# A two-layer trunk on one core: small TensorE products as alternating groups, GpSimd's arithmetic on VectorE, SwiGLU gates by tanh beside the mixers

## The chip, the cores and the metric

The kernel runs on one core of a Trainium2 chip. The metric is the device time of the program in microseconds (us). The engines are named as in the profile: PE is TensorE (PEld its weight loads), DVE is VectorE, ACT is ScalarE, POOL is GpSimd, SP is SyncE, whose queue issues the DMAs.

## The reference, cut to what matters

The input is x, 256 tokens of 1024 channels, and 256 memory tokens. Two layers are run one after the other; each is a half-weighted SwiGLU block, a mixer, and a second half-weighted SwiGLU block, each with a residual and a layer norm behind it.

```python
for i in range(DEPTH):            # 2 layers
    x = layer_norm(ALPHA * x + 0.5 * swiglu(x, ffn1...[i]), ...)
    proj = x @ w_in               # rwkv_w_in in layer 0, sb_w_in in layer 1
    mix  = rwkv7_mix(...) if i == 0 else stick_breaking_mix(...)
    heads = concatenate([mix, memory_attention(mq, mem_k, mem_v)])
    x = layer_norm(ALPHA * x + heads @ w_out[i], ...)
    x = layer_norm(ALPHA * x + 0.5 * swiglu(x, ffn2...[i]), ...)

def swiglu(x, w_gate, w_up, w_down):
    return (jax.nn.silu(x @ w_gate) * (x @ w_up)) @ w_down     # 1024 -> 2816 -> 1024
```

RWKV-7 mixing has 12 heads of 64 channels and a state of 64x64 a head, which is carried along the tokens with a decay; stick-breaking attention has 12 heads of 64 and a causal mask, and multiplies each token's weight with what earlier breaks left over; memory attention is a softmax over the 256 memory tokens with 4 heads of 64.

## The kernel before, in words

**Tiling.** The 256 tokens are two halves of 128 (`hf` 0 and 1), one token a partition. A matrix product with weights uses float32 split into a rounded high part and the rest: `piece` loads up to 128x1024 weights into a `raw` buffer, ACT makes `hi` and DVE makes `lo` = raw - hi, and each product is three fp32r products (`mm3`). There are nine `hi` and nine `lo` buffers (NPIECE) and eight `raw` ones. DVE's `lo` instructions have one line each in the profile (`lo<-raw,hi`, 128x1024).

**Feed-forward blocks.** The 2816 hidden channels are 11 blocks of 256 (`ffn_block`). A block of one half alone ("single") computes gate and up for that half with 24 products of 512 columns, gates them in `gated` (tile `h`), turns `h` with the PE (`turn_h`) and adds the down product to the accumulators of that half (`acc0` or `acc1`). A "shared" block serves both halves at once with 96 products of 256 columns and loads its weights once. A single block for each half loads the same weights twice. A single block has six weight pieces, as a shared one has.

**Order of the halves.** The two halves run out of step: while one half is in its mixer, the other half's single blocks stand beside it as work for PE. LAGS says how many blocks are single ones before and after each mixer, HEAD and HOLD and TAIL which of them run before, with, or after which step; `alternate` deals out the fill by weights in RW and SB.

**The mixers.** In `rwkv` a half is two chunks of 64 tokens (`c`), and partitions of a tile are (chunk, token) or (head parity, channel). Its products of 64 rows by 64 columns use one quarter of the PE array each. `narrow` makes head products out of `qr` and `bt`, `kq` those of `kt` and `qr`; `product` (in the loop over `_LEVELS`) inverts a triangular matrix by blocks; then a loop over the two chunks does c0 (Sk·V into `xb` and `Ov`), c1 (Tt·X into `ub`, which becomes U), the state's part (`through_state`), c3 (the new state S), and RB·U into `Ov`. In the trace Sk·V is `vn,Sk`, Tt·X is `L,Tt`, RB·U is `Lm,RB`, and the state's part is `S,qr`. In `stick` the scores z use 64 rows and 128 columns (`bn,S` and `bn,kn` in the trace), the outputs 128 rows and 64 columns. `mem_attention` has scores of 64 rows (`memKT,mq`) and outputs of 64 columns (`eT,memV`); it is called by both mixers.

**What sets the order.** Every engine runs its own queue in order. The kernel first records all operations in `Plan` (`add` with the dependencies found by `touch`, and `price` for a duration), then `order` picks, by due times, one operation after another for all engines, `improve` repeats that 24 times with shaken priorities from a random generator (SEED) and keeps the best by its own cost sheet, and `issue` writes the program in that order. So an edit to the operations or to a constant of the planner gives a new order for the whole kernel. BOOST is a bonus for the operations of a mixer's chain, SWITCH a malus for an ACT function outside the table that is loaded, AHEAD how far a queue may look ahead.

**Silu and tables.** ACT holds tables of functions; SETS in the planner has them as (Exp, Tanh), (Sigmoid, Tanh), (Ln, Exp), (Silu, Tanh). A function outside the loaded set costs a table load, which the profile shows as ACT_TABLE_LOAD.

Of the kernel before, what the change touches and what calls it, by code (L numbers as in the profile page):

```python
# [12 lines left out]
F32 = mybir.dt.float32  # L13
# [31 lines left out]
LAGS = ((5, 9), (4, 8))  # L45
# [6 lines left out]
TAIL = (3, 2)  # L52
AHEAD = dict(PE=0.0, DVE=400.0, ACT=0.0)
WAIT = 0.98
SWITCH = 392.0
BOOST = 26.25
# [46 lines left out]
class Op:  # L103
    __slots__ = ("i", "eng", "fn", "a", "k", "took", "lag", "after", "opens", "closes", "pri", "func", "port", "left",
                 "ready", "end", "users", "row", "kb", "turns", "mode", "rows", "spent", "fine")
# [18 lines left out]
SEED = 2  # L124
# [3 lines left out]
class Plan:  # L128


    def __init__(self, nc):
# [6 lines left out]
        self.index = {}  # L138
# [24 lines left out]
    def add(self, eng, fn, method, a, k):  # L163
        o = Op()
        o.i, o.eng, o.fn, o.a, o.k = len(self.ops), eng, fn, a, k
        o.pri = o.i + self.bias
        o.after = {}
# [5 lines left out]
        o.turns = [j for j, real in o.after.items() if not real]  # L173
        o.after = list(o.after)
        self.price(o, method, aps)
        self.ops.append(o)
        return o

    def touch(self, o, x, w):
# [16 lines left out]
        if psum:  # L196
            for q in range(q0, q1):
                if o.eng == "PE":
# [3 lines left out]
                    if st["pe"][q] is not None:  # L202
                        dep[st["pe"][q]] = True
# [36 lines left out]
    def price(self, o, method, aps):  # L240
        free = lambda x: int(np.prod([n for _, n in x.ap[1:]])) if len(x.ap) > 1 else 1
        sb = lambda x: x.space != PSUM
        o.func, o.port, o.row, o.kb, o.mode, o.rows = None, False, None, 0.0, None, 0
# [3 lines left out]
        if o.eng == "PE":  # L247
            out, st, mv = o.a[0], o.a[1], o.a[2]
            cols, m = free(mv), free(st)
            rows = st.ap[0][1]  # L250
            o.mode, o.rows = (rows <= 64, m <= 64), rows
            if method == "transpose":
                o.took, o.lag = 111.0, 175.0
            elif st.dtype == F32R:
                o.took, o.lag = max(cols / 2.4, m / 1.2) + 13.3, 180.0
            elif rows <= 64 and m <= 64:
                o.took, o.lag = 58.0 * max(1.0, cols / 64), 220.0
            else:
                o.took, o.lag = 2 * max(cols / 1.2, m / 1.2 + 4), 200.0
                if rows <= 64:  # L260
                    o.row = st.offset // st.ap[0][0] // 64
        elif o.eng == "ACT":
            fun = o.a[2] if len(o.a) > 2 else o.k["func"]
            o.func = {AF.Exp: "Exp", AF.Tanh: "Tanh", AF.Sigmoid: "Sigmoid", AF.Ln: "Ln", AF.Silu: "Silu"}.get(fun)
            ptr = sum(isinstance(o.k.get(x), bass.AP) for x in ("scale", "bias"))
            o.took = 95.0 + 0.845 * n + 93.0 * ptr + (92.0 if "accum_out" in o.k else 0.0)
# [28 lines left out]
    def order(self, given=()):  # L295
# [14 lines left out]
        for name, st in self.seen.items():  # L310
            if name in self.tag_of:
                ops[st["ops"][0]].opens.append(name)
                for j in set(st["ops"]):
                    ops[j].closes.append(name)
        held, self.reuse = {}, []
# [6 lines left out]
        table, landed, row = 0, 0.0, None  # L322
# [6 lines left out]
        def earliest(o):  # L329
            t = o.ready  # L330
            for n in o.opens:
                f = free[self.tag_of[n]]
                if not f:
                    return None
                t = max(t, f[0][0])
            return t

        while done < len(ops):
# [41 lines left out]
            if e == "PE":  # L380
                if t > clock["PE"] + 30:
                    t += 60.0
                if o.row is not None and row is not None and row != o.row:
                    took *= 0.55
                row = o.row
                if o.mode != mode:
                    if mode is not None:
                        t += 95.0
                        took += 108.0 * (o.a[1].dtype == F32R)
# [6 lines left out]
                share = min(o.rows, P) / P  # L396
# [111 lines left out]
    def issue(self, tc):  # L508
# [14 lines left out]
        with tc.manual_schedule():  # L523
            for _, _, o in order:
                for x in chain(o.a, o.k.values()):
# [7 lines left out]
                o.fn(*[at(x) for x in o.a], **{k: at(x) for k, x in o.k.items()})  # L533
# [3 lines left out]
def kernel(ctx, tc, const, x, mem, f1g, f1u, f1d, f2g, f2u, f2d, ln_g, ln_b, w_out, w_mem_kv,  # L537
# [60 lines left out]
    def mm3(o, sh, sl, wh, wl, start, stop):  # L598
        nc.tensor.matmul(o, sh, wh, start=start, stop=False)
        nc.tensor.matmul(o, sh, wl, start=False, stop=False)  # L600
        return nc.tensor.matmul(o, sl, wh, start=False, stop=stop)
# [13 lines left out]
    def to_T(src, dst, j0, n):  # L615

        for g in range(0, n, 4):
            m = min(4, n - g)
            pt = ps("tp")
            for i in range(m):  # L620
                nc.tensor.transpose(pt[:, i * P:(i + 1) * P], src[:, (g + i) * P:(g + i + 1) * P], ident)
# [84 lines left out]
    def ffn_block(w, c, halves):  # L706
# [42 lines left out]
        for k in range(KT):  # L749
            for f in range(2):  # L750
                for u in range(2):
                    wh, wl = (t[:, k % 2, u * FC + f * P:u * FC + (f + 1) * P] for t in gu[k // 2])
                    b = o[f][:, u * SEQ:(u + 1) * SEQ]
                    nc.tensor.matmul(b, wh, xTt[0][:, k], start=k == 0 and u == 0, stop=False)
                    nc.tensor.matmul(b, wh, xTt[1][:, k], start=False, stop=False)
                    nc.tensor.matmul(b, wl, xTt[0][:, k], start=False, stop=k == KT - 1 and u == 1)
# [36 lines left out]
    def mem_attention(hf, mqT):  # L793

        o = ps(f"acc{hf}")
        ov = o[:, :MEMW].rearrange("p (j t) -> p j t", j=2)
        rs = new(tp_, [P, 3, NMH], F32, "rs", "rs", 2)
        for p in range(2):
            sc = ps(f"acc{hf}")
            scv = sc.rearrange("p (j m) -> p j m", j=2)  # L800
            pr = slice(p * HD, (p + 1) * HD)
            two = slice(2 * p, 2 * p + 2)
            for j in range(2):
                nc.tensor.matmul(scv[:, j], mqT[pr, j], memKT[pr, j], start=True, stop=True)
# [9 lines left out]
            pt = ps("tp")  # L814
            for j in range(2):
                for m in range(2):
                    i = 2 * j + m
                    nc.tensor.transpose(pt[:, i * P:(i + 1) * P], e[:, j, m * P:(m + 1) * P], ident)
# [585 lines left out]
```

## Time and profile before

| | |
|---|---|
| median of 3 runs | 1150.29 us (1149.66 to 1152.18) |
| profiled execution | 1150.96 us, span 1149.2 us |
| PE, DVE, ACT, POOL busy | 1107.0, 932.0, 753.9, 63.6 us |
| mean granted TensorE clock | 0.990 |
| read from HBM | 301.08 MB |

Busy time is the union of an engine's instructions. Matmuls overlap in the array, so a busy PE is not a PE at its peak: for the pace of small products the start times of a run of them count, not the length of one. All instructions are issued from one line of the program (L533), so groups are told apart by their tiles: `out<-in` with the shapes, `rows*columns` of the array in front for PE.

### The profile page before, as it was taken

To read this page: it belongs to the slowest core of one execution; us is meant where nothing else is said; L and a number is where in the kernel's file an instruction comes from. 1 tells how busy PE (TensorE), PEld (TensorE's weight loads), DVE (VectorE), ACT (ScalarE), POOL (GpSimd) and SP (SyncE) were. 2 spreads that over 40 slices of the span, in tenths; PEclk is the share of its full clock that TensorE was granted. 3 is DMA by queue.
4 is the path that set the end of the run, shared out by engine and by line. 5 is a ranking of instruction groups with operands and counts; after the bars stand their busy time and mean duration, and the time that the engine had idled before them with its cause. 6 is when DMAs were issued, how large, how long until landed. Compare 5 with 4: busy or idle time off the path is not lost.

```text
span 1149.2 us, 19305 instructions
## 1 busy us (share of the span) xinstructions
PE 1107.0 (96%) x7021; PEld 932.8 (81%) x7021; DVE 932.0 (81%) x1358; ACT 753.9 (66%) x1007; POOL 63.6 (6%) x50
## 2 busy tenths in 40 slices
PE   7999999999899989999999999999999999999996
PEld 7799888877878768888887898988876776888885
DVE  5747679999799996998788955558879888997677
ACT  6545558985269863667666645447797799766562
POOL 0000000122400124000000000000100000000000
PEclk9999999999799999999999999999999999999999
DMA  9669778862658764799989986777977986999883
GB/s 353 227 233 329 259 240 306 298 211 97 207 192 290 237 184 139 238 365 342 340 272 329 315 278 191 236 226 255 368 236 247 324 284 204 369 358 298 277 281 123
DMA packets 212258, 303.42 MB, mean 264 GB/s; under 512 B 13844, under 2 KB 159424, under 8 KB 212162
## 3 DMA queue, kind: packets, MB, share of 16 engines
q1 hardware_dynamic: 212162, 302.18, 77.6%
q8 instruction: 55, 0.90, 0.3%
q14 instruction: 41, 0.34, 0.1%
HBM read 301.08 MB, written 1.05 MB: 263 GB/s over the span
## 4 chain that ended last, share of the span: by engine, by line
PE 77%; DVE 8%; DMA 5%; ACT 5%; issue 2%; POOL 1%; SPq 0%; DVEq 0%; ACTq 0%; POOLq 0%
PE ps_30r L533 24%; PE ps_29r L533 22%; PE ps_25r L533 7%; PE ps_26r L533 7%; PE ps_28r L533 6%; PE ps_27r L533 6%; PE ps_3r L533 3%; PE ps_2r L533 2%; ACT L533 1%; DVE Tt_366r L533 1%; DVE x L533 1%; DVE lo_17r L533 1%; DVE lb_506r L533 1%; DVE lo_14r L533 1%; DMA raw_24r<-in_sb_w_in_dram 1%
## 5 line engine op out<-in xcount | busy, mean ns | idle before, releaser
L533 ACT ACTIVATE h_33r<-ps_30r 128x256 f32<-128x256 f32 (+1 forms) x51 | 21.4, 420 | 55.2 <-PE ps_30r L533 53.1
L533 ACT ACTIVATE h_32r<-ps_29r 128x256 f32<-128x256 f32 (+1 forms) x49 | 19.9, 407 | 42.5 <-PE ps_29r L533 38.7
L533 ACT ACT_TABLE_LOAD x33 | 42.3, 1283 | 3.7 <-DVE rs_798r L533 1.7
L533 DVE TENSOR_TENSOR h_33r<-h_33r,ps_30r 128x256 f32<-128x256 f32 x40 | 16.7, 418 | 25.0 <-ACT h_33r L533 24.6
L533 DVE TENSOR_TENSOR h_32r<-h_32r,ps_29r 128x256 f32<-128x256 f32 x42 | 17.6, 420 | 22.6 <-ACT h_32r L533 22.3
L533 POOL COPY gup_134r<-h_32r 128x256 f32<-128x256 f32 (+1 forms) x2 | 5.5, 2755 | 371.3 <-ACT h_32r L533 352.5
L533 PE MATMUL ps_30r<-lo_8r,xTh 128*128 128x512 f32 (+1 forms) x48 | 18.8, 392 | 0.3 <-DVE lo_8r L533 0.3
L533 PE MATMUL ps_30r<-lo_17r,xTh 128*128 128x512 f32 (+1 forms) x42 | 16.8, 400 | 1.2 <-DVE lo_17r L533 1.2
L533 PE MATMUL ps_2r<-cst,x 128*128 128x128 f32 x48 | 9.4, 301 | 8.2 <-DMA x<-in_x_dram 5.4
L533 ACT ACTIVATE hi_37r<-raw_18r 128x1024 fp32r<-128x1024 f32 x12 | 12.7, 1056 | 6.8 <-issue 2.0
L533 ACT ACTIVATE hi_40r<-raw_36r 128x1024 fp32r<-128x1024 f32 x11 | 11.6, 1057 | 8.4 <-DMA raw_36r<-in_sb_w_in_dram 3.8
L533 ACT ACTIVATE hi_16r<-raw_15r 128x1024 fp32r<-128x1024 f32 x11 | 11.6, 1059 | 8.1 <-PE ps_27r L533 2.4
L533 PE MATMUL ps_30r<-hi_16r,xTh 128*128 128x512 f32 (+1 forms) x44 | 16.8, 382 | 0.0
L533 PE MATMUL ps_30r<-lo_35r,xTh 128*128 128x512 f32 x40 | 16.7, 418 | 0.0
L533 ACT ACTIVATE hi_40r<-raw_39r 128x1024 fp32r<-128x1024 f32 x14 | 14.8, 1054 | 2.7 <-PE ps_28r L533 1.5
L533 ACT ACTIVATE hi_22r<-raw_9r 128x1024 fp32r<-128x1024 f32 x12 | 12.7, 1060 | 5.7 <-PE ps_30r L533 3.1
L533 PE MATMUL ps_30r<-hi_7r,xTh 128*128 128x512 f32 (+1 forms) x42 | 16.4, 390 | 0.0
L533 PE MATMUL ps_30r<-hi_16r,xTl 128*128 128x512 f32 (+1 forms) x44 | 16.3, 371 | 0.0
L533 PE MATMUL ps_30r<-hi_7r,xTl 128*128 128x512 f32 (+1 forms) x42 | 16.2, 385 | 0.0
L533 DVE TENSOR_TENSOR xTl<-ps_2r,xTh 128x512 fp32r<-128x512 f32 (+1 forms) x15 | 10.0, 669 | 7.2 <-ACT xTh L533 7.1
L533 PE MATMUL ps_30r<-lo_14r,xTh 128*128 128x512 f32 (+1 forms) x40 | 15.4, 385 | 0.0
L533 PE MATMUL ps_29r<-hi_22r,xTl 128*128 128x512 f32 x38 | 15.3, 404 | 0.0
(1998 smaller groups left out, 4606.0 us busy)
## 6 DMA issues: line engine op xcount, KB each, us to landing
raw_24r<-in_ffn_w_down_dram SPq DMA_DIRECT2D x25, 512.0 KB, 5.1
raw_18r<-in_ffn_w_gate_dram SPq DMA_DIRECT2D x41, 256.0 KB, 4.1
raw_18r<-in_ffn_w_up_dram SPq DMA_DIRECT2D x41, 256.0 KB, 5.1
raw_12r<-in_ffn_w_gate_dram SPq DMA_DIRECT2D x36, 256.0 KB, 4.3
raw_12r<-in_ffn_w_up_dram SPq DMA_DIRECT2D x36, 256.0 KB, 6.2
raw_15r<-in_ffn_w_gate_dram SPq DMA_DIRECT2D x36, 256.0 KB, 4.0
raw_15r<-in_ffn_w_up_dram SPq DMA_DIRECT2D x36, 256.0 KB, 4.8
raw_39r<-in_ffn_w_gate_dram SPq DMA_DIRECT2D x36, 256.0 KB, 4.9
```

What stands on the lines that cost most here:

```text
L533: o.fn(*[at(x) for x in o.a], **{k: at(x) for k, x in o.k.items()})
```

## The change

1. `together` binds products into one unit of the plan, issued without anything in between; the three products of `mm3`, the transposes into one bank and the small products of a step are such units. Inside the small units the order alternates between parts of the array: `narrow` and `kq` go over (head parity, chunk) as (0,0), (1,1), (1,0), (0,1) into two banks; memory scores, z and the outputs alternate the head parity; c0 is done for both chunks at once, alternating chunks; RB·U of chunk 0 alternates with Tt·X of chunk 1.
2. The state's x part goes into banks of its own as 12 products of 64x64 for a chunk instead of 6 of 128x64 into `xb`, and DVE adds it to X.
3. All arithmetic and copies of POOL move to DVE; POOL keeps its memsets.
4. Beside a mixer a single block is gated with tanh: silu(g)·u = 0.5·g·(1 + tanh(g/2))·u, one ACT instruction and two DVE instructions instead of Silu and one multiply. BESIDE says where.
5. Planner: `price` knows the places of a product in the array; the special price for alternating rows goes; constants as in the diff.

```diff
-LAGS = ((5, 9), (4, 8))
+LAGS = ((5, 9), (5, 8))
...
-TAIL = (3, 2)
-AHEAD = dict(PE=0.0, DVE=400.0, ACT=0.0)
+TAIL = (2, 2)
+AHEAD = dict(PE=100.0, DVE=400.0, ACT=0.0)
 WAIT = 0.98
-SWITCH = 392.0
-BOOST = 26.25
+SWITCH = 49.0
+BOOST = 18.375
+BESIDE = (True, False)
...
-SEED = 2
+SEED = 201
...
+    @contextmanager
+    def together(self):
+        self.bundle = []
+        yield
+        o, self.bundle = self.bundle[0], None
+        self.close(o)
...
     def mm3(o, sh, sl, wh, wl, start, stop):
-        nc.tensor.matmul(o, sh, wh, start=start, stop=False)
...
+        with nc.together():
+            nc.tensor.matmul(o, sh, wh, start=start, stop=False)
...
         def gated(dst, g, u):
-            nc.scalar.activation(dst, g, AF.Silu)
-            nc.vector.tensor_tensor(dst, dst, u, ALU.mult)
+            if beside:
+                nc.scalar.activation(dst, g, AF.Tanh, scale=0.5)
+                nc.vector.scalar_tensor_tensor(dst, dst, 1.0, g, ALU.add, ALU.mult)
+                nc.vector.scalar_tensor_tensor(dst, dst, 0.5, u, ALU.mult, ALU.mult)
+            else:
...
     def mem_attention(hf, mqT):
+        banks = [ps(f"acc{hf}").rearrange("p (j m) -> p j m", j=2) for p in range(2)]
+        with nc.together():
+            for j in range(2):
+                for p, pr in enumerate(rows):
+                    nc.tensor.matmul(banks[p][:, j], mqT[pr, j], memKT[pr, j], start=True, stop=True)
...
+        with nc.together():
             for j in range(2):
                 for m in range(2):
+                    for p, pr in enumerate(rows):
+                        h = 2 * j + p
+                        nc.tensor.matmul(ov[pr, j], memV[:, m, h * HD:(h + 1) * HD], turned_e[p][:, j, m], start=m == 0, stop=m == 1)
...
-            nc.gpsimd.tensor_tensor(Lm, L, bc(lvl[:, l], 1, [P, NH, C]), ALU.mult)
+            nc.vector.tensor_tensor(Lm, L, bc(lvl[:, l], 1, [P, NH, C]), ALU.mult)
...
+        with nc.together():
+            for i in range(NH):
+                for cs in both:
+                    nc.tensor.matmul(xb[i // 6][cs, i % 6], Sk[cs, i, 0], V[cs, i], start=i % 6 == 0, stop=i % 6 == 5)
+        nc.scalar.activation(X[:, 0:6], xb[0], AF.Copy)
+        nc.vector.tensor_copy(X[:, 6:12], xb[1])
...
+        for c, cs in enumerate(both):
             first = hf == 0 and c == 0
+            if not first:
+                xs = six("tp")
+                with nc.together():
+                    for j in range(NT):
+                        for p in range(2):
+                            pr = slice(p * HD, (p + 1) * HD)
+                            nc.tensor.matmul(xs[p][cs, j], qr[pr, j, 0, cs], S[pr, j, p], start=True, stop=True)
+                for p in range(2):
+                    nc.vector.tensor_tensor(par(X)[cs, :, p], par(X)[cs, :, p], xs[p][cs], ALU.add)
...
+            with nc.together():
+                for i in range(NH):
+                    nc.tensor.matmul(ub[i // 6][cs, i % 6], Tt[cs, i], X[cs, i], start=True, stop=True)
+                    if c == 1:
+                        nc.tensor.matmul(Ov[i // 6][both[0], i % 6], RB[both[0], i], U[both[0], i], start=False, stop=i % 6 == 5)
...
-        run(blocks(w, solo(1, range(HEAD))))
-        alternate(chain_steps(mixer(0, mixed)), blocks(w, solo(1, range(HEAD, lag1))), steps)
+        run(blocks(w, solo(1, range(HEAD)), BESIDE[0]))
+        alternate(chain_steps(mixer(0, mixed)), blocks(w, solo(1, range(HEAD, lag1)), True), steps)
...
-        alternate(second, blocks(w, solo(0, range(lag2 - HOLD[i]))), steps)
-        run(chain_steps(mixed_out(1, mixed[1], w_out[i])), blocks(w, solo(0, range(lag2 - HOLD[i], lag2))))
+        alternate(second, blocks(w, solo(0, range(lag2 - HOLD[i])), True), steps)
+        run(chain_steps(mixed_out(1, mixed[1], w_out[i])), blocks(w, solo(0, range(lag2 - HOLD[i], lag2)), BESIDE[1]))
```

More of the change, by code (lines that the diff above doesn't have):

```diff
@@ L3 @@
 import random
+from contextlib import contextmanager
 from itertools import chain
@@ L103 @@
 class Op:
-    __slots__ = ("i", "eng", "fn", "a", "k", "took", "lag", "after", "opens", "closes", "pri", "func", "port", "left",
-                 "ready", "end", "users", "row", "kb", "turns", "mode", "rows", "spent", "fine")
+    __slots__ = ("i", "eng", "calls", "took", "lag", "after", "opens", "closes", "pri", "func", "port", "left", "ready",
+                 "end", "users", "kb", "turns", "mode", "share", "spent", "fine", "parts", "round", "places")
 class Engine_:
@@ L137, in __init__, with close @@
             (("PE", "tensor"), ("DVE", "vector"), ("ACT", "scalar"), ("POOL", "gpsimd"), ("SP", "sync")))
-        self.index = {}
+        self.index, self.bundle = {}, None
+    @contextmanager
[4 more added lines that the diff above has]
+        self.close(o)
+    def close(self, o):
+        o.turns = [j for j, real in o.after.items() if not real]
+        o.after = list(o.after)
+        if o.eng != "PE":
+            return
+        free, t, work = {}, 0.0, 0.0
+        for took, places, share in o.parts:
+            t = max([t] + [free.get(x, 0.0) for x in places])
+            free.update((x, t + took) for x in places)
+            work += took * share
+        o.took = max(free.values())
+        o.share = min(1.0, work / o.took)
     def slot(self, pool, shape, dtype, tag, name, bufs):
@@ L172, in add @@
                 self.touch(o, x, w)
[L173 to L176, printed above, removed]
+        self.price(o, method, aps, a, k)
+        if not self.bundle:
+            self.close(o)
         return o
@@ new lines, in rwkv @@
+        six = lambda tag: [ps(tag)[:, :384].rearrange("q (i t) -> q i t", i=6) for _ in range(2)]
+        both = [slice(c * C, (c + 1) * C) for c in range(2)]
+        xb, Ov = six("tp"), six(ac)
+        with nc.together():
+            for i in range(NH):
[3 more added lines that the diff above has]
+        nc.vector.tensor_copy(X[:, 6:12], xb[1])
@@ L1168, in rwkv @@
             nc.scalar.activation(U[cs, 0:6], ub[0][cs], AF.Copy, scale=-1.0)
             nc.vector.tensor_scalar(U[cs, 6:12], ub[1][cs], -1.0, None, ALU.mult)
-            through_state(Ov, 1, False)
+            if not first:
+                with nc.together():
+                    for j in range(NT):
+                        nc.tensor.matmul(Ov[j // 3][cs, 2 * (j % 3):2 * (j % 3) + 2].rearrange("q h d -> q (h d)"), qr[:, j, 1, cs],
+                                         S[:, j].rearrange("p a d -> p (a d)"), start=False, stop=False)
@@ L1186, in rwkv @@
                     yield "c3"
+        with nc.together():
             for i in range(NH):
-                nc.tensor.matmul(Ov[i // 6][cs, i % 6], RB[cs, i], U[cs, i], start=False, stop=i % 6 == 5)
+                nc.tensor.matmul(Ov[i // 6][both[1], i % 6], RB[both[1], i], U[both[1], i], start=False, stop=i % 6 == 5)
         hs = new(tp_, [P, 2, NH], F32, "hs", "hs", 2)
@@ L1324, in spread, with blocks @@
         return [(c, h) for _, c, h in sorted(seq, key=lambda t: t[0])]
-    def blocks(w, seq):
+    def blocks(w, seq, beside=False):
         waiting = []
         for c, halves in seq:
-            hidden = yield from ffn_block(w, c, halves)
+            hidden = yield from ffn_block(w, c, halves, beside)
             yield from chain(*waiting)
```

288 lines of the change are left out of this document (142 added, 146 removed).

## The prediction

> **What bounds the kernel now.** I read the page first: part 1 (busy shares), part 2 (the span in slices) and part 4 (the chain that ended last).
>
> ```profile
> PE 1107.0 (96%) x7021; PEld 932.8 (81%) x7021; DVE 932.0 (81%) x1358; ACT 753.9 (66%) x1007; POOL 63.6 (6%) x50
> DVE  5747679999799996998788955558879888997677
> PEclk9999999999799999999999999999999999999999
> PE 77%; DVE 8%; DMA 5%; ACT 5%; issue 2%; POOL 1%; SPq 0%; DVEq 0%; ACTq 0%; POOLq 0%
> ```
>
> PE carries the span, but the 81% of DVE is a mean: in slices 7 to 16 and again late it stands at 9. So I asked for busy time by stages: 200 to 650 us holds both RWKV mixers and what surrounds them, 800 to 1050 the two stick-breaking mixers. Columns: PE, PEld, DVE, ACT, POOL busy, clock, DMA share, GB/s.
>
> ```profile
> 200.00:325.00 125.00, 116.58 (x1130) 96.60 (x1129) 112.83 (x234) 79.58 (x127) 29.51 (x22) 0.95 0.59 196
> 325.00:475.00 150.00, 144.46 (x1240) 117.38 (x1239) 134.94 (x252) 102.49 (x156) 24.15 (x14) 1.00 0.66 214
> 475.00:650.00 175.00, 172.02 (x898) 144.68 (x898) 156.49 (x207) 117.90 (x147) 0.00 (x0) 1.00 0.93 321
> ...
> sum 700.00, PE 675.28 PEld 550.27 DVE 623.72 ACT 502.75 POOL 61.70; mean PE 112.55 PEld 91.71 DVE 103.95 ACT 83.79 POOL 10.28
> 350.00:400.00 50.00, 48.31 (x313) 39.27 (x311) 49.35 (x100) 45.19 (x73) 4.93 (x3) 1.00 0.77 255
> 650.00:800.00 150.00, 150.00 (x953) 136.10 (x953) 98.43 (x122) 81.76 (x106) 0.00 (x0) 1.00 0.75 244
> ```
>
> The sum row is for six stages, 700 us in all. There PE is 96.5% busy (675.28/700) and DVE 89.1% (623.72/700). In 650 to 800, which is feed-forward work alone, PE is full and DVE at 66%. The change touches only the 700 us, so the forecast is made there: what PE no longer needs, what DVE needs more, and which of the two is then the longer.
>
> **PE: the grouped small products.** The timeline prints runs of equal instructions as one row: start, length, count. A float32 product leaves two records, so x24 is a bank of 12 products.
>
> ```profile
> 309.93 0.91 PE L533 MATMUL ps_26r<-Lm_367r,RB_370r 64*64 64x64 f32 x12
> 440.58 0.92 PE L533 MATMUL ps_2r<-Tt_366r,Lm_367r 64*64 64x64 f32 x23
> 281.00 0.22 PE L533 MATMUL ps_26r<-Y_377r,T_376r 64*64 64x64 f32 x1
> 452.99 0.51 PE L533 MATMUL ps_3r<-vn_347r,kn_346r 64*64 64x64 f32 x11
> 253.45 1.20 PE L533 MATMUL ps_25r<-Lm_367r,qr_56r 64*64 64x64 f32 x24 [0.21 <-ACT h_32r L533]
> 268.48 0.92 PE L533 MATMUL ps_25r<-qr_56r,bn_442r 64*64 64x128 f32 x12
> 828.88 1.13 PE L533 MATMUL ps_26r<-memKT,mq_365r 64*128 64x256 f32 x4
> 851.76 0.93 PE L533 MATMUL ps_26r<-bn_442r,S_136r 64*128 64x128 f32 x6
> 853.28 1.09 PE L533 MATMUL ps_25r<-eT_1732r,memV 128*64 128x128 f32 x8
> 447.80 0.82 PE L533 MATMUL ps_3r<-S_136r,qr_56r 128*64 128x128 f32 x6
> 303.75 1.54 PE L533 MATMUL ps_3r<-S_136r,qr_56r 128*64 128x128 f32 x6
> 966.95 0.44 PE L533 MATMUL ps_28r<-Sk_381r,gup_134r 128*64 128x128 f32 x4
> ```
>
> One record alone is 0.22 us, its tail included, so the pace is (length - 0.22)/(count - 1). The first row stays in one quarter of the array (rows and columns of one chunk): 63 ns a record. The second is `product`, which already alternates two quarters: 32 ns. The fourth (c3) keeps its rows and alternates column halves: 29 ns. So alternation of quarters and of columns is worth a factor of two, shown. Alternation of row halves with all columns (memory scores, z) or one column half (the state's part) is not shown by any row. Its ends are no gain and a factor of two; I take the factor, since the quarters, which change row and column half together, are the nearest row.
>
> The terms, with counts from the code over both halves: c0's Sk·V, 192 records from 63 to 32: 6.0 us. c1: RB·U of chunk 0 rides beside Tt·X of chunk 1, 96 records at 32 instead of 63: 3.0. `kq`, 96 records at 64 (fifth row from 268.48) to 32: 3.1. `narrow`, 192 records at 43, already alternating columns, to 32: 2.1; its low end is zero. The state's x part, 36 records at 120 become 72 small ones at 32: 2.0 (low end zero: one column half, and at 63 it would be slightly worse, -0.2). Memory scores, 32 records at 300 to 150: 4.8. Memory output, 64 at 124 to 62: 4.0. z, 72 at 140 to 70: 5.0. The stick output already runs at 73 ns (last row) in mixed order: nothing. Sum 30.0; with only the kinds whose alternation is shown (6.0 + 3.0 + 4.0) it is 13.0. The row at 303.75 is the same six records as that at 447.80 at half clock; the clock of 200 to 325 is 0.95, so at most 125 x 0.05 = 6.3 us more comes back where denser work keeps the clock up. I leave that out of the sum and keep it for the range.
>
> The Trainium skill, TensorE: Matmul & The Clock Gate, Part 3 (the mechanism), says that a weight load overlaps a running matmul only when the row group differs. By that rule the memory output would gain nothing and the sum would be 26.0. The c3 row, which keeps its rows and still goes at 29 ns, speaks against it here, and I follow the row.
>
> **DVE: what comes to it.**
>
> ```profile
> L533 POOL TENSOR_TENSOR Lm_367r<-L_382r,cst 128x768 f32<-128x768 f32 x4 | 6.8, 1701 | 20.2 <-PE ps_2r L533 10.5 <-PE ps_3r L533 9.7
> L533 POOL TENSOR_TENSOR T_376r<-T_376r,g_373r 128x768 f32<-128x768 f32 x2 | 3.6, 1812 | 7.3 <-DMA T_376r<-in_rwkv_lnx_g_dram 7.3
> L533 DVE TENSOR_TENSOR qr_56r<-kn_346r,T_376r 128x768 f32<-128x768 f32 x2 | 1.9, 953 | 0.0
> L533 DVE TENSOR_TENSOR lo_14r<-raw_18r,hi_19r 128x1024 fp32r<-128x1024 f32 x6 | 7.3, 1223 | 0.5 <-ACT hi_19r L533 0.5
> 446.29 2.49 DVE L533 TENSOR_TENSOR lo_14r<-raw_9r,hi_40r 128x1024 fp32r<-128x1024 f32 x1
> L533 DVE SCALAR_TENSOR_TENSOR Y_377r<-Tt_366r,cst,Y_377r 128x256 f32<-128x256 f32 x1 | 0.5, 486 | 0.6 <-POOL Y_377r L533 0.6
> L533 DVE TENSOR_TENSOR h_32r<-h_32r,ps_29r x42: 411/421/424, 20.7 to 1129.4; 128x256 f32<-128x256 f32 x42
> L533 DVE COPY L_382r<-ps_2r 64x384 f32<-64x384 f32 x3 | 1.7, 558 | 2.1 <-PE ps_2r L533 2.1
> L533 ACT ACT_TABLE_LOAD x33 | 42.3, 1283 | 3.7 <-DVE rs_798r L533 1.7 <-PEq L1392 0.7 <-DVE rs_489r L533 0.6
> DVE h_32r L533 <- ACT h_32r L533: 25.9, 23, 3.6
> ```
>
> POOL's eight groups of 768 columns are 18 instructions; on DVE one takes 953 ns: 17.1 us. Six of 256 columns at 421 are 2.5; the four copies of V (256 and 512) at the same rate 2.5; eight tiny ones at 0.17 (estimate from rows of 12 columns, 1.4). Together 23.5. Against it: a DVE instruction that meets POOL is longer, as the one at 446.29 (2.49 against 1.22). In the mixers twelve are longer than their like in this way, by some 10.8 us in all (estimate over the trace: 0.3 to 1.4 each); that goes. Ends: 0 and 10.8; I take 10.8, because POOL keeps memsets alone.
>
> Tanh gating: layer 0 has 2 + 3 + 7 single-half blocks beside a mixer, layer 1 2 + 3 + 5, together 22. In each one multiply (421) becomes two three-operand instructions (486 each): 22 x 0.551 = 12.1. X: four copies of 64 rows (558) go; two of 128 rows and six adds come at about the same length: +2.2. These adds sit between the state's product and Tt·X, 0.55 us more in the chain of three chunks; Tt·X and behind it U wait for them. Ride: Ov of chunk 0 closes one chunk later, with nobody waiting but the norm at the end. lag1 of layer 1 from 4 to 5 turns one shared block into two single ones: its six weight pieces are loaded and split once more, 6 x 1.22 = 7.3 us of DVE, ten more issues on SP's queue ahead of later weights (3 MB; at the 196 to 321 GB/s of the stage rows 10 to 16 us of transfer, beside other work where the DMA share is below 0.93). TAIL and HOLD move blocks, not work. Sum for DVE: 23.5 - 10.8 + 12.1 + 2.2 + 7.3 = +34.3.
>
> On PE that lag is even, by two rows of the chain:
>
> ```profile
> 499.29 5.44 PE ps_30r L533 x24
> 645.55 2.64 PE ps_30r L533 x22
> ```
>
> Two single blocks are 48 records of 512 columns at 227 ns, 10.9 us, a shared one 96 of 256 at 120, 11.5, and the single ones add four transposes.
>
> ACT loses table loads: 31 of the 33 fall into the mixers. If half go, 20 us less of 502.75 in 700 and 6 us more of splitting. ACT was no bound, so I count it at nothing; the cover is PE's other work, and where DVE waits for the gate (last row, 25.9 us) it can only shorten.
>
> The new order itself (seed, weights of the planner, and three-product groups that can't be cut, 3 x 0.227 = 0.68 us that a small product may have to wait behind) has no row. I bound it by one point of the bound engine's share each way, 7 us of 700, take nothing for it, and keep the 7 us in the range.
>
> **Sum.** PE needs 675.3 - 30.0 = 645.3 us of the 700, DVE 623.7 + 34.3 = 658.0. DVE overtakes PE. Today's bound runs at 96.5% of the stretch, and 350 to 400 shows DVE itself at 98.7%; so I give DVE 96.5%: 658.0/0.965 = 682, which is 18 us less. The profiled execution took 1150.96 us (span 1149.2), 0.7 over the median of 1150.29. 1150.96 - 18 = 1133; on the median 1132.
>
> **Rivals.**
> A, the other side: DVE can't be packed so tightly. It waits for ACT (last row above) and is in order, so that the moved arithmetic queues behind splits of 1.22 us. At 92% the stretch is 658/0.92 = 715, 15 us more: 1165. It loses from 94.0% downward (658/700). For it: 89.1% now, ACT's waits. Against: 98.7% in the busiest 50 us, and that today's idle DVE time is PE's doing. Beside it stands the Trainium skill, TensorEngine Tiling (Array Packing), PSUM Bottleneck: faster small products leave emptying the PSUM as the limit. Chance 0.20.
> B: splits slide out of the mixers into stages like 650 to 800 where DVE is at 66%, and PE stays the bound: 645.3/0.965 = 669, 31 us less: 1120; with the clock's 6 us, 1114. Against: nine weight buffers hold 9 x 1.22 = 11 us of splitting. Chance 0.24.
> C: the grouping does not do what it says. The order of now already mixes products of different quarters, and half-rows may not overlap; PE's gain is 13 or less (662 or more needed) with DVE at 658. Two engines so close share at 95%: 697, 1148. Chance 0.12, of it half within 0.2%.
> The forecast (1122 to 1146) has 0.44.
>
> 0.2% of this kernel, about 2.3 us, is what a measurement of it can tell from none. Faster: 0.44 + 0.24 + 0.05 = 0.73. Same: 0.06 of C and 0.02 of A, 0.08. Slower: 0.19. The range 1112 to 1156 leaves out the far part of A (above 1156) and some of B; its likeliest part is 1122 to 1146.
>
> **What would show it.** c0, c1, scores and z rows near half their length per record: right; scores unchanged: row halves don't overlap, and PE gains 13 to 18. POOL below 5 us and no split over 2 us: contention gone. DVE near 966 us in all and above 95% in the two stretches: DVE is the bound; near 90% with PE still at 97%: rival B. PE's share below 93% in 200 to 650 with DVE below 94%: rival A. Table loads near 17. The clock at 1.00 in 200 to 325: the 6 us came. The forecast is wrong if DVE's added work is not 34 us, or if its share there stays under 94%.

## The result and the profile after

The changed kernel takes 1132.09 us (median of four runs); the kernel before took 1150.96 on the same chip. The ratio is 0.9836 [0.9815, 0.9856], so it is 18.9 us faster. The profiled execution took 1131.83 us, its span is 1129.7. The forecast of 1132 was met, but not by the way that it gave: two of its errors cancelled, which is luck.

From the page of the changed kernel: busy time by engine, the slices of DVE and of the clock, the chain's shares, and the group of table loads.

```profile
PE 1075.0 (95%) x7013; PEld 903.4 (80%) x7013; DVE 955.0 (85%) x1426; ACT 739.3 (65%) x991; POOL 2.7 (0%) x14
...
DVE  6747669999999899999879965569889999998777
...
PEclk9999999998889889999999999999999999999999
...
PE 83%; DVE 12%; issue 2%; DMA 2%; ACT 1%; SPq 0%; DVEq 0%; ACTq 0%
...
L562 ACT ACT_TABLE_LOAD x13 | 16.7, 1283 | 0.9 <-PEq L1451 0.7
```

PE has 32.0 us less to do, DVE 23.0 more, POOL next to nothing, ACT 20 table loads fewer. PE's idle time rose from 42.2 to 54.7 us (span less busy): of the 32.0 us that PE saved, 12.5 came back as waiting, and the span fell by the other 19.5. The clock has five slices at 8, where before it had one at 7.

Stages cut by the clock on the wall don't hold the same work in two kernels. I therefore cut both where PE has issued the same large products (128 rows by 128 columns, at 227 ns for 512 columns and 120 for 256). From 200 to 500 us of these lies the RWKV stretch, from 640 to 800 the stick-breaking stretch. Busy time by stretch, first before, then after; columns as in the prediction (length, PE, PEld, DVE, ACT, POOL, clock, DMA share, GB/s):

```profile
230.40:676.00 445.60, 428.65 (x3274) 357.32 (x3273) 395.08 (x651) 286.73 (x402) 49.78 (x31) 0.98 0.75 254
819.20:1037.90 218.70, 211.14 (x1059) 166.36 (x1058) 190.70 (x251) 180.42 (x232) 3.15 (x3) 0.99 0.86 294
```

```profile
229.60:669.80 440.20, 410.21 (x3306) 338.17 (x3305) 405.42 (x693) 275.33 (x390) 1.05 (x5) 0.96 0.76 257
813.20:1019.70 206.50, 200.69 (x1056) 159.47 (x1055) 192.43 (x262) 165.11 (x219) 0.00 (x0) 0.99 0.90 309
```

This is the reading that matters most. In the stick stretch PE saves 10.5 us and the stretch is 12.2 shorter. In the RWKV stretch PE saves 18.4 and the stretch is only 5.4 shorter, because PE's idle time there rises from 17.0 to 30.0; DVE got 10.3 more there and the clock fell from 0.98 to 0.96. The rest of the program moved by 1.9.

The mean over 440 us hides a change of places. Two windows in which the small products of RWKV lie, cut on the wall clock and so only roughly the same work, first before, then after:

```profile
250.00:350.00 100.00, 91.87 (x947) 76.39 (x947) 89.72 (x179) 52.58 (x84) 19.44 (x13) 0.93 0.54 177
400.00:450.00 50.00, 46.15 (x577) 37.72 (x575) 43.04 (x83) 27.06 (x42) 14.24 (x9) 1.00 0.55 172
```

```profile
250.00:350.00 100.00, 85.15 (x958) 69.03 (x957) 95.17 (x194) 50.73 (x79) 0.64 (x3) 0.88 0.60 198
400.00:450.00 50.00, 42.55 (x625) 33.44 (x625) 48.45 (x100) 24.97 (x39) 0.00 (x0) 0.93 0.58 194
```

Here DVE does overtake PE (95 to 97% against 85%). In the 200 us behind them, 450 to 650, PE is at 99% and DVE at 92%.

The small products themselves, in the timeline (start, length, count):

```profile
284.45 0.87 PE L562 MATMUL ps_26r<-vn_347r,Sk_381r 64*64 64x64 f32 x24
...
402.17 0.23 PE L562 MATMUL ps_3r<-qr_56r,Lm_367r 64*64 64x64 f32 x2
402.18 0.26 PE L562 MATMUL ps_27r<-qr_56r,Lm_367r 64*64 64x64 f32 x2
402.23 0.23 PE L562 MATMUL ps_3r<-qr_56r,Lm_367r 64*64 64x64 f32 x2
...
814.77 0.38 PE L562 MATMUL ps_26r<-memKT,mq_365r 64*128 64x256 f32 x1
814.78 0.38 PE L562 MATMUL ps_25r<-memKT,mq_365r 64*128 64x256 f32 x1
814.99 0.38 PE L562 MATMUL ps_26r<-memKT,mq_365r 64*128 64x256 f32 x1
...
827.02 0.27 PE L562 MATMUL ps_26r<-eT_1733r,memV 128*64 128x128 f32 x1
827.03 0.27 PE L562 MATMUL ps_26r<-eT_1736r,memV 128*64 128x128 f32 x1
827.13 0.27 PE L562 MATMUL ps_26r<-eT_1733r,memV 128*64 128x128 f32 x1
...
830.14 0.27 PE L562 MATMUL ps_25r<-bn_442r,S_136r 64*128 64x128 f32 x1
830.15 0.27 PE L562 MATMUL ps_26r<-bn_442r,S_136r 64*128 64x128 f32 x1
830.25 0.27 PE L562 MATMUL ps_25r<-bn_442r,S_136r 64*128 64x128 f32 x1
```

c0 goes at (0.87 - 0.22)/23 = 28 ns a record instead of 63. `narrow` (the rows at 402 us) starts four records each 0.06 us: 15 ns a record instead of 43, all four quarters at once. Memory scores come in pairs 0.01 us apart, a pair each 0.22 us: 110 ns a record in the middle of a run, where before they were 216 apart. Memory outputs and z come in pairs each 0.10 to 0.11 us: some 53 ns instead of 109 and 112. Counted from the first start to the start of the next product, first and last record included, scores went from 264 to 133 ns a record, z from 144 to 72, memory outputs from 127 to 64.

So two row halves with all their columns do run at the same time. The trace of before had two places that show it, which the prediction overlooked: where two groups of z stood behind each other, some of their records started in pairs, and they took 99 ns a record.

```profile
936.80 0.27 PE L533 MATMUL ps_27r<-bn_442r,S_136r 64*128 64x128 f32 x1
936.81 0.27 PE L533 MATMUL ps_28r<-bn_442r,kn_346r 64*128 64x128 f32 x1
```

The longest waits of PE in the RWKV stretch, of the kernel before (one row) and of the changed one (us in total, times, longest):

```profile
PE ps_2r L533 <- DVE x L533: 2.3, 2, 1.8
...
PE ps_29r L562 <- DVE lo_14r L562: 7.1, 2, 6.0
PE ps_2r L562 <- DVE lb_506r L562: 5.9, 1, 5.9
PE ps_26r L562 <- DVE Y_377r L562: 5.8, 1, 5.8
```

The longest three take 6.0, 5.9 and 5.8 us, 17.7 together, more than the 13.0 by which PE's idle time rose in this stretch. Before, the longest was 1.8.

Two of the three, from 256.3 and from 403.0 us, lie in the run of 30 short DVE instructions, each on the result of the one ahead of it, that inverts the 16-wide blocks of the triangle. In DVE's queue what PE needs stands behind most of them: a split (`lo_14r`, started at 261.04, although PE had read its `hi_13r` at 255.89), and the two gate instructions of `h_33r`, which end at 408.78. The row names `lb_506r` because that run uses this buffer; it is not the bonus arithmetic that came from POOL, and these instructions were on DVE before the change too. In the third, from 306.0, PE wants to write the bank `ps_26r` again, and DVE empties it (`Y_377r`) behind splits and a norm.

Next, what goes with such waits: windows of the changed kernel just ahead of four places where the granted clock halves, and one of the halved stretches itself.

```profile
255.10:258.50 3.40, 1.19 (x7) 0.66 (x4) 2.99 (x13) 1.71 (x3) 0.00 (x0) 1.00 0.29 116
258.60:268.80 10.20, 6.49 (x38) 4.72 (x39) 9.89 (x31) 2.55 (x4) 0.00 (x0) 0.50 0.22 78
292.70:296.10 3.40, 1.98 (x48) 1.61 (x44) 2.94 (x9) 0.78 (x1) 0.00 (x0) 1.00 0.45 152
...
302.90:306.30 3.40, 1.61 (x36) 1.47 (x36) 3.29 (x5) 0.97 (x2) 0.00 (x0) 1.00 0.61 195
...
374.60:378.00 3.40, 1.98 (x11) 1.41 (x10) 3.40 (x6) 1.94 (x2) 0.00 (x0) 1.00 0.73 252
```

Each time PE is busy for 1.2 to 2.0 of 3.4 us while DVE is busy for 2.9 to 3.4, and then PE goes at half clock. In these pockets DVE is the bound. It is no sharp rule: in the kernel before PE was busy for 1.73 of the 3.4 us from 314.2, and the clock stayed whole.

A half clock costs only where PE has work. The halved stretches of the changed kernel add up to 45 us, and PE is busy in 28.2 of them; before, it was in 16.5 of 23. So half of that, 8.3 us before and 14.1 after, was added to PE's busy time by the clock, as an estimate: 5.8 us more. The mean clock (0.9901 and 0.9800) makes it look like 11.2, for it also counts stretches in which PE waits for DVE, and the end of the program, where PE has nothing left. The Trainium skill, TensorE: Matmul & The Clock Gate, Part 1 (The HAM clock gate), says that the gate follows how busy PE was in windows of about 3.4 us; the trace agrees, with halved stretches of 3.4, 6.8 and 10.2 us in the mixers.

### The profile page after: what moved, and what is told of

Read it like the earlier page. It is cut to its first block, busy times and chain, and to the rows that moved or that the text cites. A ratio compares the mean times of both kernels' runs of the same rounds, so it can differ in the third digit from the quotient of the medians.

```text
span 1129.7 us, 19266 instructions
## 1 busy us (share of the span) xinstructions
PE 1075.0 (95%) x7013; PEld 903.4 (80%) x7013; DVE 955.0 (85%) x1426; ACT 739.3 (65%) x991; POOL 2.7 (0%) x14
## 4 chain that ended last, share of the span: by engine, by line
PE 83%; DVE 12%; issue 2%; DMA 2%; ACT 1%; SPq 0%; DVEq 0%; ACTq 0%
PE ps_29r L562 25%; PE ps_30r L562 25%; PE ps_28r L562 7%; PE ps_27r L562 7%; PE ps_26r L562 7%; PE ps_25r L562 7%; PE ps_2r L562 3%; PE ps_3r L562 3%; DVE Y_377r L562 1%; DVE Tt_366r L562 1%; DVE lo_17r L562 1%; DVE lo_35r L562 1%; DVE lo_14r L562 1%; DVE lo_23r L562 1%; DMA raw_9r<-in_ffn_w_up_dram 1%
## 5 line engine op out<-in xcount | busy, mean ns | idle before, releaser
L562 ACT ACTIVATE h_32r<-ps_30r 128x256 f32<-128x256 f32 (+1 forms) x50 | 21.1, 421 | 30.3 <-PE ps_30r L562 29.8
L562 ACT ACTIVATE h_33r<-ps_29r 128x256 f32<-128x256 f32 (+1 forms) x48 | 20.0, 416 | 31.1 <-PE ps_29r L562 30.8
L562 PE MATMUL ps_30r<-hi_16r,xTh 128*128 128x512 f32 x46 | 19.7, 428 | 0.0
L562 PE MATMUL ps_30r<-lo_17r,xTh 128*128 128x512 f32 x46 | 18.1, 393 | 1.0 <-DVE lo_17r L562 1.0
L562 PE MATMUL ps_2r<-cst,x 128*128 128x128 f32 x48 | 9.2, 325 | 10.3 <-DMA x<-in_x_dram 5.3
L562 PE MATMUL ps_30r<-hi_16r,xTl 128*128 128x512 f32 x46 | 18.0, 392 | 0.0
L562 PE MATMUL ps_30r<-hi_10r,xTh 128*128 128x512 f32 (+1 forms) x42 | 17.5, 416 | 0.0
L562 PE MATMUL ps_29r<-hi_22r,xTh 128*128 128x512 f32 x42 | 17.4, 415 | 0.0
L562 ACT ACTIVATE hi_16r<-raw_36r 128x1024 fp32r<-128x1024 f32 x10 | 10.6, 1057 | 10.2 <-DMA raw_36r<-in_w_out_dram 9.0
L562 DVE TENSOR_TENSOR lo_23r<-raw_9r,hi_22r 128x1024 fp32r<-128x1024 f32 x12 | 14.6, 1218 | 3.0 <-ACT hi_22r L562 3.0
L562 PE MATMUL ps_30r<-lo_11r,xTh 128*128 128x512 f32 (+1 forms) x42 | 16.5, 394 | 0.3 <-DVE lo_11r L562 0.3
L562 PE MATMUL ps_29r<-lo_23r,xTh 128*128 128x512 f32 x42 | 16.6, 395 | 0.0
L562 PE MATMUL ps_30r<-hi_10r,xTl 128*128 128x512 f32 (+1 forms) x42 | 16.5, 392 | 0.0
L562 DVE TENSOR_TENSOR lo_35r<-raw_12r,hi_34r 128x1024 fp32r<-128x1024 f32 x12 | 14.6, 1216 | 1.9 <-ACT hi_34r L562 1.9
```

The costliest lines, as they stand in the source:

```text
L562: fn(*[at(x) for x in a], **{n: at(x) for n, x in k.items()})
```

## The experiments

The question was which engine sets the time now. The prediction says DVE; the rival is that PE still does. Every run was timed beside the kernel before, on one chip; the changed kernel itself was not run again on the chips of the other runs, so a difference from it goes over two ratios. All differences in us below are ratios times 1150.5, about the time before.

**More work for one engine, in both kernels.** One more copy of a split for each single block beside a mixer (22 in the changed kernel, 21 before, 1.22 us each), or two more bundles of three large products for each (132 and 126 records of 227 ns).

```diff
 # piece(): more DVE work (a_dve, b_dve)
         made.append(nc.vector.tensor_sub(lo, raw, hi.bitcast(F32)))
+        if again:
+            made.append(nc.vector.tensor_sub(lo, raw, hi.bitcast(F32)))
 # ffn_block(): more PE work (a_pe, b_pe)
+                if beside and k == 0:
+                    for _ in range(2):
+                        mm3(o, xT[hf][0][:, k], xT[hf][1][:, k], wh[:, k % 2], wl[:, k % 2], True, True)
                 yield mm3(o, ...)
```

> The changed kernel with one of the six weight splits of each of the 22 single blocks beside a mixer done twice on DVE (the same result): 22 x 1.22 = 27 us more DVE work, no more PE work. Theory 1 (in the changed kernel DVE sets the time beside the mixers): +15 to +27 us, 1147 to 1159. Theory 2 (PE still sets it, and what is missing of the 30 us was lost to the coarser units and the new order): +0 to +8 us, 1132 to 1140.

> The changed kernel with the first three products of each of the same 22 single blocks done three times instead of once (the same result): 22 x 6 x 0.227 = 30 us more PE work, no more DVE work. Theory 1 (DVE sets the time there): part of it is hidden, +8 to +20 us, 1140 to 1152. Theory 2 (PE sets it): +25 to +32 us, 1157 to 1164.

> The kernel before with the same doubled split in its 21 single blocks at the same places: 26 us more DVE work. Theory 1 says that before the change PE set the time there and DVE had 11% idle: less than in the changed kernel, +3 to +14 us, 1154 to 1165. Theory 2 makes no difference between the two kernels: +0 to +8.

> The kernel before with the same tripled products in its 21 single blocks: 29 us more PE work. Both theories: nearly all of it, +24 to +31 us, 1175 to 1182; theory 1 says clearly more than the same load costs in the changed kernel.

| run | ratio to the kernel before | costs | of what was added |
|---|---|---|---|
| a_dve | 0.9937 [0.9916, 0.9958] | 11.6 us over the changed kernel | 26.8 us of DVE: 0.43 |
| a_pe | 0.9974 [0.9960, 0.9987] | 15.9 us over the changed kernel | 30.0 us of PE: 0.53 |
| b_dve | 1.0125 [1.0109, 1.0141] | 14.4 us over the kernel before | 25.6 us of DVE: 0.56 |
| b_pe | 1.0168 [1.0151, 1.0185] | 19.3 us over the kernel before | 28.6 us of PE: 0.67 |

With the intervals of both ratios the two shares of DVE are 0.31 to 0.56 and 0.49 to 0.64, and those of PE 0.44 to 0.62 and 0.61 to 0.74. Each run is also a new order, and another order of the changed kernel alone moved it by 4.4 us (seed2 below), some 0.16 of what was added. Against the busy time by which the engine really rose (20.9, 27.3, 29.6 and 23.5 us, in the order of the table), the shares are 0.56, 0.58, 0.49 and 0.82.

DVE did not become the bound of the whole: had it, its added work would cost nearly all of itself, and more than before. The costs of a_dve, b_pe and, by 0.4 us, b_dve lie in none of the ranges that were expected; that of a_pe lies in Theory 1's. Before the change PE's work was the dearer; now both engines cost about half of what is added to them, because the two take turns at being late. By stretch (a_dve, then b_dve):

```profile
229.30:676.60 447.30, 411.85 (x3309) 335.83 (x3308) 415.28 (x702) 275.51 (x392) 1.05 (x5) 0.97 0.75 253
819.90:1031.80 211.90, 203.66 (x1056) 160.10 (x1055) 200.93 (x272) 168.00 (x223) 0.00 (x0) 0.98 0.88 303
```

```profile
230.90:688.80 457.90, 433.92 (x3273) 360.63 (x3272) 412.05 (x664) 288.63 (x403) 50.52 (x32) 0.97 0.73 247
831.70:1052.90 221.20, 212.77 (x1059) 167.28 (x1058) 200.53 (x260) 182.05 (x233) 2.93 (x3) 0.98 0.85 294
```

In the RWKV stretch DVE's added busy time costs about 0.7 of itself in both kernels (7.1 for 9.9; 12.3 for 17.0, although nine of the added splits, 11 us, lie in this stretch in either kernel). In the stick stretch it costs 5.4 for 8.5 now and 2.5 for 9.8 before. Each figure is from one profiled execution, and another order moves a stretch by some 3 us (437.3 in seed2 for 440.2); by these DVE counted in the RWKV stretch before the change too, which a mean over 700 us hid.

**The alternation undone (serial).** The units stay, and within them the order is by quarter or row half, one after the other:

```diff
-                for j in range(NT):
-                    for p, c in ((0, 0), (1, 1), (1, 0), (0, 1)):
+                for p, c in ((0, 0), (0, 1), (1, 0), (1, 1)):
+                    for j in range(NT):
 # likewise in the second of these loops, memory scores and outputs, c0, the state's x part, RB·U, z and stick outputs
```

> The changed kernel with its units kept, but the small products of each unit in the order that stays in one quarter or half as long as it can (narrow, kq, memory scores and outputs, c0, the state's x part, z, the stick outputs; RB after Tt instead of beside it). Undoes the alternation alone. Theory 1: PE needs some 28 us more but DVE sets the time, so about +10 to +22 us, 1142 to 1154. Theory 2 (PE is the bound): +25 to +32, 1157 to 1164. If alternation was worth nothing: no change.

1137.76 us, 0.9873 [0.9851, 0.9896]: 4.3 us slower than the changed kernel, with intervals that overlap. Its page and its stretches:

```profile
PE 1093.9 (96%) x7013; PEld 925.1 (81%) x7013; DVE 957.8 (84%) x1426; ACT 738.0 (65%) x991; POOL 2.7 (0%) x14
```

```profile
230.90:674.70 443.80, 422.59 (x3307) 351.88 (x3306) 408.61 (x694) 275.58 (x391) 1.05 (x5) 0.98 0.76 255
818.20:1026.90 208.70, 204.49 (x1056) 164.80 (x1055) 195.27 (x264) 165.82 (x220) 0.00 (x0) 0.99 0.90 309
```

That is less than either range that was expected. The alternation saves 18.9 us of PE's busy time, and 11.6 of them come back as idle time of PE (43.1 in serial, 54.7 after); in the RWKV stretch 12.4 us bring 3.6. The clock there is 0.98 without it and 0.96 with it. Starts to starts say the same: all products but the large ones, each counted to the next start and to 0.33 us at most, take 158.1 us in serial and 137.3 after, 20.8 less, and what is left beyond them and the usual pace of the large ones rises by some 13. So most of what alternation saves comes back as waits and half clock.

Not all of the faster products need the alternation. The memory scores run in the same pairs in serial, at 134 ns a record to the next product for 133 with it and 264 before: it is enough that the two row halves stand behind each other in one unit. z takes 99 there and memory outputs 94, between before (144, 127) and after (72, 64).

**One part put back at a time.** `silu` gates by Silu everywhere, `pool_back` returns the moved arithmetic to POOL, `group_only` does both, so that the groups and the planner's constants alone are left.

```diff
 # silu, group_only
-            if beside:
+            if False:
                 nc.scalar.activation(dst, g, AF.Tanh, scale=0.5)
 # pool_back, group_only; likewise the other 13 instructions
-            nc.vector.tensor_tensor(Lm, L, bc(lvl[:, l], 1, [P, NH, C]), ALU.mult)
+            nc.gpsimd.tensor_tensor(Lm, L, bc(lvl[:, l], 1, [P, NH, C]), ALU.mult)
```

> The changed kernel with Silu and one multiply in all blocks, as before. DVE has some 9 us less, ACT some 20 table loads of 1.28 us more. Theory 1 as a sum: -3 to -9 us; if ACT's table loads lie in the mixers' chains: slower, +3 to +12 us. Theory 2: +-3 us.

> The changed kernel with the 36 arithmetic instructions and copies of GpSimd back on GpSimd. DVE loses 23 us of work and gets back up to 11 us of contention, so 12 us less by net. Theory 1 (DVE sets the time): if only the sum counts, -5 to -12 us, 1120 to 1127; if GpSimd's longer instructions (1.7 to 2.7 us against 0.95) in the chain cost more than DVE's work, slower by up to 8. Theory 2: within 3 us.

> The grouping alone, with the changed kernel's planner and lags: GpSimd's work on GpSimd and Silu as before. If the three parts add up, its time is the changed kernel's plus the sum of the differences of the two runs before; DVE then has 21 us less work than in the changed kernel, so theory 1 as a sum gives -8 to -20 us, 1112 to 1124, and a time above 1135 says that latency of GpSimd and of the table loads, not DVE's sum, was what these two parts removed.

silu: 1133.88 us, 0.9839 [0.9818, 0.9861]. pool_back: 1139.32, 0.9884 [0.9859, 0.9910]. group_only: 1137.98, 0.9875 [0.9852, 0.9898]. Their stretches, in this order:

```profile
229.80:663.80 434.00, 405.99 (x3309) 336.41 (x3308) 403.15 (x682) 280.25 (x395) 1.05 (x5) 0.96 0.77 261
807.50:1021.20 213.70, 203.84 (x1057) 159.04 (x1056) 189.72 (x254) 179.61 (x233) 0.00 (x0) 0.99 0.85 296
```

```profile
231.00:680.30 449.30, 415.87 (x3309) 344.08 (x3308) 404.05 (x668) 275.99 (x389) 47.66 (x31) 0.95 0.76 253
823.70:1031.00 207.30, 201.88 (x1057) 160.60 (x1057) 192.00 (x259) 166.42 (x221) 6.29 (x3) 0.98 0.89 307
```

```profile
229.90:668.50 438.60, 409.71 (x3310) 335.42 (x3309) 401.61 (x663) 283.85 (x397) 49.70 (x31) 0.97 0.78 259
812.10:1026.00 213.90, 203.44 (x1056) 159.32 (x1055) 190.10 (x251) 179.52 (x233) 2.70 (x3) 0.99 0.86 296
```

pool_back is 5.5 us slower than the changed kernel although DVE has 3.1 us less to do, and group_only 4.5 slower although it has 9.6 less: less work for DVE in sum did not make the kernel faster. By time silu shows nothing, 0.3 us. By stretch it shows two things that cancel. With tanh the stick stretch is 206.5, 207.3 and 208.7 us long (after, pool_back, serial), with Silu 213.7 and 213.9: tanh seems worth some 6 us there, where it takes 14 us off ACT; but `consts` below, with tanh and the old constants, is at 212.7. With tanh the RWKV stretch is 440.2 instead of 434.0, and with POOL in its old place 449.3 instead of 438.6: some 6 to 11 us lost, part of which is the order: the same operations as after take 437.3 in seed2, so that 3 is as likely as 6. The move from POOL to DVE shortens the RWKV stretch by 4.6 (group_only to silu) to 9.1 us (pool_back to after) and leaves the stick stretch alone, where POOL had little. The groups with the constants take 7.0 and 4.8 us off the two stretches (before to group_only), and 14.4 us off the time.

**Order and constants.** The seed and the planner's constants changed together with the operations. `seed2` is the changed kernel with the old seed, `consts` the changed operations with all the old constants and seed, `b_consts` the kernel before with the new ones.

```diff
 # seed2
-SEED = 201
+SEED = 2
 # consts: that, and LAGS, TAIL, AHEAD, SWITCH and BOOST as before; b_consts: the reverse, in the kernel before
```

> The changed kernel with the planner's seed 2 instead of 201 and nothing else: another order of the same instructions. It shows how far the order alone moves the time, which every run here that edits an operation moves as well. If orders are alike: within 3 us of the changed kernel, ratio 0.981 to 0.987. If the seed was a good part of the gain: +4 to +10 us, ratio 0.987 to 0.992.

> The changed kernel's operations, units and price sheet with the planner's constants, lags and seed of before (LAGS layer 1 at 4, TAIL 3, AHEAD 0, SWITCH 392, BOOST 26.25, seed 2). If the operations carry the gain: ratio 0.981 to 0.989, within 5 us of the changed kernel. If the constants carry it: 0.992 to 1.000. Theory 1 (DVE sets the time) adds that one shared block instead of two single ones takes 7 us off DVE, so that it might even be as fast.

> The kernel before with the changed kernel's constants, lags and seed and none of its operations. If the constants carry a part of the gain that needs no new operation: ratio 0.990 to 0.996. If they only suit the new operations: 1.000 to 1.010.

seed2: 1128.93 us, 0.9798 [0.9785, 0.9812]. consts: 1136.30, 0.9865 [0.9852, 0.9879]. b_consts: 1151.15, 0.9989 [0.9980, 0.9998]. So the new constants do next to nothing for the old operations (1.3 us, in neither expected range), the new operations bring 15.5 us with the old constants, and with the new operations the constants are worth 7.7 more at seed 2. seed2 is faster than both kernels, by 4.4 us against the changed one, with the same work on every engine, which neither expected range had; its mean clock is 0.984 to 0.985 in all runs, that of the changed kernel 0.978 to 0.981.

**DVE relieved (act).** Copies of DVE, nine us by their lengths as estimated, go to ACT, which is at 65%.

```diff
-        nc.vector.tensor_copy(X[:, 6:12], xb[1])
+        nc.scalar.activation(X[:, 6:12], xb[1], AF.Copy)
 # likewise, in the mixers, the copies of turned memory weights, mq and the last column, and one scaling by a lane mask
```

> The changed kernel with nine us of copies and scalings of the RWKV mixers moved from DVE to ACT, which is half idle there: the memory attention's turned weights, the first half of X, the lane products, the shift's first columns, lastc, mq. Theory 1 (DVE sets the time there): -5 to -9 us, ratio 0.976 to 0.980. By what the doubled split cost (11.6 us for 27, so 0.43 of it): -4 us, 0.980. If DVE doesn't set it: within the spread of orders.

1133.33 us over five runs, 0.9823 [0.9803, 0.9844]: 1.5 us better than the changed kernel, inside the uncertainty. DVE's busy time fell by 5.2 us (955.0 to 949.8), not by nine, and 0.43 of that is 2.2. Another reading tells more: the five runs are one program, and they took 1127.20 and 1129.34 us at a mean clock of 0.985 and 0.984, and 1133.33, 1133.70 and 1133.97 at 0.980, 0.980 and 0.978. Time and clock go together; whether the clock made the time, or a late product made both, is not shown, for only one of the five has a trace.

## Why the prediction was right, and where it was not

**PE's saving: right in sum.** 30.0 us were forecast; PE's busy time fell by 32.0, although more half clock added some 5.8 to it, and from start to start, counted as in serial, the small products fell from 164.8 to 137.3 us, by 27.4. The factor of two for row halves, taken from the quarters without a row of its own, was there; only for memory scores the forecast's 300 to 150 was 264 to 133, as the last of these records is 0.38 us long and not 0.22. Memory outputs, which keep their rows and alternate column halves, halved too: the rule of the Trainium skill in TensorE: Matmul & The Clock Gate, Part 3, that was weighed in the prediction, does not hold for them. The state's x part came as forecast where nothing held it up (24 records from 453.39 to 454.24, 35 ns each to the next product, for 12 at 121 before). `narrow` brought 192 x (43 - 15) = 5.4 us instead of 2.1.

**DVE's added work: mis-sized, +23.0 for +34.3.** The runs that add one part after another split the 23.0, by the busy time of DVE on their pages:

| step | DVE busy, us | rise | forecast |
|---|---|---|---|
| before to b_consts (constants; one shared block as two single ones) | 932.0 to 940.4 | 8.4 | 7.3 |
| to group_only (units, the X adds) | to 945.4 | 5.0 | 2.2 |
| to silu (POOL's work on DVE) | to 948.8 | 3.4 | 23.5 - 10.8 = 12.7 |
| to the changed kernel (gates by tanh) | to 955.0 | 6.2 | 12.1 |

POOL's work was the largest miss. Each instruction costs what was forecast (949 ns below, for 953), but what DVE no longer loses to POOL is more: the lengths of the 36 moved instructions add up to 22 us, those of all others fall by some 13 (from pool_back to the changed kernel), and lengths overstate busy time, since successive records overlap: over the whole kernel they add up to 1037 us for 955.0 busy. The 546 splits alone take 664.6 us where 540 took 663.7, and the longest is 1.23 us instead of 2.49. For the gate the forecast took 486 ns for each of the two new instructions, from a row that reads SBUF alone; with one operand in PSUM they take 412, less than the multiply that goes:

```profile
L562 DVE SCALAR_TENSOR_TENSOR h_33r<-h_33r,ps_29r 128x256 f32<-128x256 f32 x20 | 8.2, 412 | 0.1
L562 DVE TENSOR_TENSOR h_33r<-h_33r,ps_29r 128x256 f32<-128x256 f32 x31 | 13.0, 418 | 11.3 <-ACT h_33r L562 11.1
L562 DVE TENSOR_TENSOR Lm_367r<-L_382r,cst 128x768 f32<-128x768 f32 x4 | 3.8, 949 | 0.0
```

By lengths that is 22 x (2 x 0.412 - 0.418) = 8.9 us, not 12.1.

**"DVE overtakes PE" and the 96.5%: the step that failed.** By the prediction's own sign (DVE above 95% in the stretches, wrong below 94%), DVE is at 405.42/440.20 = 92.1% and 192.43/206.50 = 93.2%, and PE at 93.2% and 97.2%. Adding to DVE costs no larger a share than before. DVE overtakes PE in the windows of the small products alone (250 to 350 and 400 to 450); over the rest PE stays the longer. Of DVE's 23.0 us only 12.1 fall into the two stretches; the forecast laid all of its term there. With DVE's true +23 the forecast's own formula would have been (623.7 + 23.0)/0.965 = 670, 30 us less; the span fell by 19.5. Too large a term for DVE stood in for a loss that the sum did not have: the 12.5 us by which PE's idle time rose, in the pockets in which PE waits for DVE. That the two come out at the same time is luck.

The prediction had the clock only as a possible gain of 6 us, with 1.00 in 200 to 325 as its sign. It went the other way: 0.90 there, for 0.95 before. Shorter small products leave PE less busy in the very windows in which DVE is full; that this is the reason is supported by serial (mean clock 0.989 for 0.980), but the order plays a part too (0.984 in seed2).

**The rivals.** B fails: no split slid out (201 and 114 of them lie in the two stretches, before and after), and PE waits up to 6.0 us for DVE. A's sign (PE below 93%, DVE below 94%) is nearly met in the RWKV stretch and not at all in the stick stretch; one of the three longest waits is for a bank that DVE empties late. C's premise is false, for the grouping works; its remark that two engines so close share at 95% is nearest to what happened: in the two stretches together PE's 610.9 us are 94.5% and DVE's 597.8 are 92.4% of 646.7.

**The rest.** Table loads: 13 for 17, and ACT's share of the chain from 5% to 1%; by itself that was worth little, as ACT was no bound outside the stick stretch. Order and seed: a bound of 7 us each way was taken, and seed2 and consts lie 4.4 below and 3.3 above the changed kernel in ratio, so the bound was needed and about right.

**Open.** How much of tanh's loss in the RWKV stretch is the gate and how much the order that came with it: no run holds the order. A kernel with tanh beside the stick mixer alone and Silu beside RWKV, which the stretches suggest, was not run; nor one in which splits and gates are put between the instructions of the block inversion earlier. And serial, without alternation, is still 14.6 us faster than the kernel before: how that divides among the units, c0 for both chunks at once, the emptied POOL and the price sheet was not separated.

## What to carry to other kernels

Where two engines are both above 90%, don't forecast with the larger of two sums and a share taken from the old bound: cut the program at the same work in each stretch, and add work to each engine in turn; here each microsecond cost about half of itself on either. When products get shorter beside an engine that is full, price the clock too: here pauses of PE of 1.4 to 2.2 us in 3.4 were followed by 3 to 10 us at half clock, though not always; and count only the half clock in which PE has work. Look up by time what DVE was doing in the longest waits: the row names the last releaser, and in two of three it was a long run of dependent instructions that everything else stood behind. A part that shows 0.3 us in the total can be a gain in one stretch and a loss in another, so judge parts by stretch, and set the size against what another order of the same work does there.

## What the runs showed of the hardware

Products of 64 rows in both row halves, with all 128 columns, run in pairs 0.01 us apart, into different banks (z at 72 ns a record to the next product instead of 144). Memory scores did so in serial too, where the records of one row half stand ahead of those of the other. Products of 64x64 that go over all four quarters start four records each 0.06 us (15 ns a record). c0 writes one bank from both row halves in turn and still goes at 28 ns. A three-operand DVE instruction of 128x256 took 412 ns with one operand in PSUM, against 486 in the row with SBUF operands alone. One and the same program ran at 1127 us with a mean clock of 0.985 and at 1134 with 0.978. In four places the clock halved after a window of 3.4 us in which PE was busy for 1.2 to 2.0, so without a pause as long as the window ahead of it.
